# Where the activations begin in SBUF: one tile for both halves of hT, 80 bytes in front of the weights modulo 512

## The chip, the cores and the metric

The kernel runs on one core of a Trainium2 chip. The metric is the device time of one execution in microseconds. The times shown are medians over runs; a profile is one execution of the program, taken by the hardware profiler.

## The reference: what is computed

A decoder trunk of two layers over 512 positions of width 1024, all in float32. Layer 0 mixes positions with three groups of dilated attention heads, layer 1 with a gated linear recurrence (RG-LRU). Each mixer is followed by a gated FFN with a short causal convolution, and each of these four blocks has a norm ahead of it and one behind it.

```python
for layer in range(DEPTH):
    j = layer // 2
    h = rms_norm(x, norm_mix_pre[layer])
    if layer % 2 == 0:
        h = dilated_attention_mixer(h, attn_w_qkv[j], attn_w_o[j], rel_bias)
    else:
        h = rglru_mixer(h, lru_w_in[j], ...)
    x = x + rms_norm(h, norm_mix_post[layer])
    h = rms_norm(x, norm_ffn_pre[layer])
    h = conv_ffn(h, ffn_w_up[layer], ffn_conv_w[layer], ffn_conv_b[layer], ffn_w_down[layer])
    x = x + rms_norm(h, norm_ffn_post[layer])
```

## The kernel before

**Products in three parts.** Weights and activations are split into a rounded part and the rest (`hi`, `lo`, both of type fp32r), and `mm3` (lines 245 to 248) sums hi x hi, hi x lo and lo x hi into one bank of PSUM. Each line is one matmul with its own weight load; the profile shows the three as L246, L247 and L248. ScalarE makes `hi` and VectorE makes `lo` (lines 146 and 147).

**Which operand is which.** A matmul has a stationary operand (loaded first, 128 columns, 512 bytes of a partition) and a moving one (streamed, up to 512 columns, 2048 bytes). There are four kinds of three-part products, named by their PSUM tile:

- `ps`: projections of the normed activations (QKV, FFN up, LRU in). Stationary is a weight slice, moving is `hT`, the transposed activations. For the first four weight units of the two FFNs and of the LRU (four banks of PSUM each time) the 512 positions are taken in two halves of 256.
- `v`: the attention's values. Stationary is a slice of `hT`, moving is the weight.
- `acc`: the projections back (attention out, LRU out, FFN down). Stationary is a slice of an activation from the general pool, moving is the weight.
- `gate`: the LRU's gates. Stationary is a weight, moving an activation from the general pool.

Beside them the attention has plain fp32 products (`S`, `O`) and transposes (`tr`, `PT`, `OT`).

**Tiles and pools.** SBUF is handed out by pools, one behind the other in the order in which they are opened: `cp` (constants, x, gains, columns), `htp` (`hT`), `wp` (raw weights, and eight units of `hi` and `lo`), `gp` (28 general tiles of 2048 bytes), `sp` (small ones). `hT` is two tiles of 16384 bytes in a partition, one for `hi` and one for `lo`, with 8 slices of 512 positions each (line 278); one pair is live at a time, and each stage's pair takes the same place. All sizes ahead of the small tiles in `htp`, `wp` and `gp` are multiples of 512 bytes, so within these pools every slice that a matmul reads begins at the same place modulo 512.

**Order of the work.** Every engine's instructions stand in the order in which the program text writes them. A pump (`pump`, `load`) keeps three raw weight loads ahead on the SP queue and splits them into units as room comes free, between the matmul groups; the norms and the attention's softmax run as side steps between groups (`tick`).

Of the kernel before, what the change touches and what calls it, by code (L numbers as in the profile page):

```python
# [11 lines left out]
F32 = mybir.dt.float32  # L12
F32R = mybir.dt.float32r
# [5 lines left out]
P = 128  # L19
S = 512  # L20
D = 1024
KD = D // P
# [12 lines left out]
GEN_BUFS = 28  # L35
TOE_BUFS = 2
CP_PAD = 8

SHORT_ORDER = [
    ([0, 1], [0, 1, 2]), ([0], [3]), ([2, 3], [0]), ([1], [3]), ([2, 3], [1]), ([2], [2, 3]), ([3], [2, 3]),  # L40
# [36 lines left out]
def kernel(  # L77
# [31 lines left out]
    cp = ctx.enter_context(tc.tile_pool(name="cp", bufs=1))  # L109
    twice = cp.tile([P, CP_PAD], F32, tag="pad", name="pad")  # L110
    htp = ctx.enter_context(tc.tile_pool(name="htp", bufs=1))
    wp = ctx.enter_context(tc.tile_pool(name="wp", bufs=W_UNITS))
    gp = ctx.enter_context(tc.tile_pool(name="gp", bufs=GEN_BUFS))
    sp = ctx.enter_context(tc.tile_pool(name="sp", bufs=8))
    pp = ctx.enter_context(tc.tile_pool(name="pp", bufs=8, space=bass.MemoryType.PSUM))
    dp = ctx.enter_context(tc.tile_pool(name="dp", bufs=1, space=bass.MemoryType.DRAM))

    uid = [0]

    def nm(s):  # L120
        uid[0] += 1
        return f"{s}{uid[0]}"
# [152 lines left out]
        return [ap[:, 0:512], ap[:, 512:1024]]  # L275

    def new_hT():
        return tuple(htp.tile([P, KD, S], F32R, tag=f"hT{i}", name=nm(f"hT{i}")) for i in range(2))

    def prenorm(t, hT, g, wait):  # L280
        xh, gh = halves(x_sb[:, t, :]), halves(g)
# [126 lines left out]
    def rows_run(nchunks, A, prep, seq, order, post, pre):  # L408
        post_g = gain(*post)
        pre_g, hT = (gain(*pre), new_hT()) if pre is not None else (None, None)  # L410
        W, banks = {}, {}
        left = {}
# [95 lines left out]
    def ffn(layer, hT, post, pre):  # L508
        ca, cc = ffn_cols[layer]

        def conv(ps, j):
            u = gen(s="u")
            nc.scalar.activation(  # L513
                u, ps, AF.Identity, scale=cc[:, j : j + 1], bias=cc[:, 48 + j : 49 + j]
            )
            for d, wc in ((1, ca[:, 48 + j : 49 + j]), (2, ca[:, j : j + 1])):
                nc.vector.scalar_tensor_tensor(  # L517
                    u[:, d:], ps[:, : S - d], wc, u[:, d:], op0=ALU.mult, op1=ALU.add
                )
            return u  # L520

        gv = []

        def sink(b, ps, j):
            m = b % 2
            if b < 2:
                u = conv(ps, 2 * j + m)
                nc.scalar.activation(u, u, AF.Gelu_apprx_tanh)  # L528
                gv.append(u)
            else:  # L530
                u = conv(ps, 24 + 2 * j + m)
                nc.vector.tensor_tensor(gv[2 * j + m], gv[2 * j + m], u, op=ALU.mult)

        order = [([0, 1, 2, 3], range(9)), ([0], range(9, 12)), ([1], range(9, 12))]
        order += [([2, 3], [9]), ([2], [10, 11]), ([3], [10, 11])]
        prep, run = rows_proj(12, act_split(gv), order, post, pre)
        for j in range(12):
            if j == 11:
                prep(3)
            feat_tiles(2, hT, lambda b, ps: sink(b, ps, j), j == 0)  # L540
        return run()
# [408 lines left out]

    root_table()
    hT = new_hT()
    nc.sync.dma_start(x_sb[:, 0, :], x[0, 0:P, :])
    g = gain(norm_mix_pre, 0, nc.sync)
# [27 lines left out]
    hT = attention(hT, (norm_mix_post, 0), (norm_ffn_pre, 0))  # L982
    hT = ffn(0, hT, (norm_ffn_post, 0), (norm_mix_pre, 1))
    hT = lru(hT, (norm_mix_post, 1), (norm_ffn_pre, 1))
# [30 lines left out]
```

## Time and profile before

| | |
|---|---|
| median of 3 runs | 1498.67 us (1498.09 to 1500.18) |
| the profiled execution's own time | 1498.71 us |
| its span, first to last instruction | 1496.9 us |
| mean granted TensorE clock | 0.997 |
| TensorE, VectorE, ScalarE busy | 1474.0, 795.3, 633.7 us |
| matmuls in the trace | 7083 |
| weight load of 1 MB, issue to landing | 5.2 us |
| fp32r matmuls that read hT | 4128 of 512 columns, 576 of 256 |

A group's line in the profile reads: line, engine, operation, output<-inputs, shapes, count | busy us, mean ns of one | idle time ahead of them and what ended it. A row of the timeline reads: start in us, length in us, engine, line, operation, names, shapes, count. Matmuls overlap, so their lengths add up to more than the time they take; the distance from start to start is what one costs. A window's row gives the length of a stretch, then each engine's busy time with its count of instructions, the granted clock, the DMA share and GB/s.

### The profile page before, as it was taken

How to read it: one execution, taken by the hardware profiler on the slowest of the kernel's cores; microseconds unless marked ns; L12 is line 12 of the kernel's file. 1: busy time of each engine (PE TensorE's matmuls, PEld its weight loads, DVE VectorE, ACT ScalarE, POOL GpSimd, SP SyncE). 2: the span in 40 equal slices, each digit the busy share in tenths (PEclk: the TensorE clock that was granted, in tenths of full speed). 3: DMA queues.
4: the chain of work that ended last, by engine and by line, in shares of the span. 5: the costliest groups of instructions: out<-in, count | busy, mean ns of one | idle time of the engine just before them, and what ended most of it. 6: DMA issues, size and time to landing. Idle time of an engine off the chain costs nothing.

```text
span 1496.9 us, 18111 instructions
## 1 busy us (share of the span) xinstructions
PE 1474.0 (98%) x7083; PEld 1237.8 (83%) x7083; DVE 795.3 (53%) x1612; ACT 633.7 (42%) x1287; POOL 43.7 (3%) x73
## 2 busy tenths in 40 slices
PE   6999999999999999999999999999999999999998
PEld 4788888888888898888888888988898888888886
DVE  6434334343434586555555336877876555565333
ACT  5334333333334554333344334579554333344321
POOL 3111000000000000000000000000000000000000
PEclk9999999999999999999999999999999999999999
DMA  6543222423334233323233231342233232323301
GB/s 215 184 164 98 92 88 85 133 100 125 107 121 137 95 110 119 106 87 111 85 113 113 85 113 43 99 142 84 85 99 113 92 105 87 110 85 116 109 1 56
DMA packets 116101, 157.64 MB, mean 105 GB/s; under 512 B 5087, under 2 KB 97463, under 8 KB 116016
## 3 DMA queue, kind: packets, MB, share of 16 engines
q1 hardware_dynamic: 111120, 145.24, 29.3%
q0 software_dynamic: 4896, 11.26, 2.3%
q8 instruction: 55, 0.90, 0.3%
q14 instruction: 30, 0.25, 0.0%
HBM read 150.14 MB, written 11.05 MB: 108 GB/s over the span
## 4 chain that ended last, share of the span: by engine, by line
PE 88%; ACT 5%; DVE 4%; DMA 2%; issue 1%; SPq 0%; POOL 0%; DVEq 0%; ACTq 0%; POOLq 0%
PE ps L246 17%; PE ps L248 17%; PE ps L247 17%; PE acc L248 7%; PE acc L246 7%; PE acc L247 7%; PE v L246 3%; PE v L247 3%; PE v L248 3%; DVE wlo L147 2%; DVE xb L838 1%; ACT whi L146 1%; PE S L714 1%; PE tr L297 1%; PE O L772 1%; PE O L699 1%
## 5 line engine op out<-in xcount | busy, mean ns | idle before, releaser
L246 PE MATMUL ps<-hT,whi 128*128 128x512 f32 (+1 forms) x1376 | 518.5, 377 | 0.0
L248 PE MATMUL ps<-hT,wlo 128*128 128x512 f32 (+1 forms) x1376 | 515.2, 374 | 0.0
L247 PE MATMUL ps<-hT,whi 128*128 128x512 f32 (+1 forms) x1376 | 515.1, 374 | 0.0
L147 DVE TENSOR_TENSOR wlo<-raw,whi 128x512 fp32r<-128x512 f32 x504 | 328.1, 697 | 270.3 <-ACT whi L146 270.1
L146 ACT ACTIVATE whi<-raw 128x512 fp32r<-128x512 f32 x504 | 285.2, 623 | 135.0 <-PE acc L248 120.9
L246 PEld LDWEIGHTS ps<-hT,whi 128*128 128x128 f32 x1376 | 259.1, 188 | 47.0 <-ACT qk L590 0.6
L248 PEld LDWEIGHTS ps<-hT,wlo 128*128 128x128 f32 x1376 | 259.0, 188 | 46.5
L247 PEld LDWEIGHTS ps<-hT,whi 128*128 128x128 f32 x1376 | 259.1, 188 | 45.6
L517 DVE SCALAR_TENSOR_TENSOR u<-ps,cols,u 128x511 f32<-128x511 f32 x192 | 143.8, 749 | 140.4 <-ACT u L513 137.0
L248 PE MATMUL acc<-whi,alo 128*128 128x512 f32 x512 | 199.4, 389 | 1.0 <-DVE alo L147 1.0
L246 PE MATMUL acc<-whi,ahi 128*128 128x512 f32 x512 | 200.0, 391 | 0.0
L247 PE MATMUL acc<-wlo,ahi 128*128 128x512 f32 x512 | 199.2, 389 | 0.0
L513 ACT ACTIVATE u<-ps,cols 128x512 f32<-128x512 f32 x96 | 74.8, 780 | 209.9 <-PE ps L248 209.9
L248 PEld LDWEIGHTS acc<-whi,alo 128*128 128x128 f32 x512 | 96.1, 188 | 21.4 <-DVE alo L147 1.4
L246 PEld LDWEIGHTS acc<-whi,ahi 128*128 128x128 f32 x512 | 96.1, 188 | 19.7
L247 PEld LDWEIGHTS acc<-wlo,ahi 128*128 128x128 f32 x512 | 96.1, 188 | 19.6
L246 PE MATMUL v<-whi,hT 128*128 128x512 f32 x192 | 78.3, 408 | 0.0
L247 PE MATMUL v<-wlo,hT 128*128 128x512 f32 x192 | 76.5, 398 | 1.4 <-DVE wlo L147 1.4
L248 PE MATMUL v<-whi,hT 128*128 128x512 f32 x192 | 76.3, 398 | 0.5 <-DVE hT L302 0.5
L528 ACT ACTIVATE u<-u 128x512 f32<-128x512 f32 x48 | 30.3, 632 | 80.6 <-DVE u L517 80.6
L651 DVE CUSTOM_DVE_ANT_0 L<-S,toe 128x128 f32<-128x128 f32 (+1 forms) x96 | 25.2, 320 | 53.4 <-DMA toe<-skew 22.7
L590 ACT ACTIVATE qk<-ps 128x512 f32<-128x512 f32 x24 | 14.3, 597 | 88.7 <-PE ps L248 76.9
(169 smaller groups left out, 1028.5 us busy)
## 6 DMA issues: line engine op xcount, KB each, us to landing
raw<-in_ffn_w_up_dram SPq DMA_DIRECT2D x48, 1024.0 KB, 5.2
raw<-in_attn_w_qkv_dram SPq DMA_DIRECT2D x28, 1024.0 KB, 5.1
raw<-in_ffn_w_down_dram SPq DMA_DIRECT2D x24, 1024.0 KB, 4.9
raw<-in_attn_w_qkv_dram SPq DMA_DIRECT2D x16, 512.0 KB, 4.9
raw<-in_lru_w_in_dram SPq DMA_DIRECT2D x8, 1024.0 KB, 5.4
skew<-rowv POOLq DMA_DIRECT2D x3, 1536.0 KB, 12.3
vrows<-v SPq DMA_DIRECT2D x16, 256.0 KB, 2.8
vp<-vrows SPq DMA_DIRECT2D x16, 256.0 KB, 4.0
```

What stands on the lines that cost most here:

```text
L146: nc.scalar.activation(hi, raw, AF.Copy)
L147: nc.vector.tensor_tensor(lo, raw, hi.bitcast(F32), op=ALU.subtract)
L246: mm(dst, l[0], r[0], start=start, stop=False)
L247: mm(dst, l[0], r[1], start=False, stop=False)
L248: mm(dst, l[1], r[0], start=False, stop=stop)
L297: nc.tensor.transpose(ps[:, k * P : (k + 1) * P], xs[i][:, k * P : (k + 1) * P], ident)
L513: nc.scalar.activation(u, ps, AF.Identity, scale=cc[:, j : j + 1], bias=cc[:, 48 + j : 49 + j])
L517: nc.vector.scalar_tensor_tensor(u[:, d:], ps[:, : S - d], wc, u[:, d:], op0=ALU.mult, op1=ALU.add)
L528: nc.scalar.activation(u, u, AF.Gelu_apprx_tanh)
L651: nc.vector.tensor_tensor_reduce(dst, ps, bias, scale=1.0, scalar=3 * NEG, op0=ALU.add, op1=ALU.max, accum_out=mx)
L699: mm(po[:, a * P : (a + 1) * P], pts[a, j], vtile(v, a - 1 + j, h % 4), start=j == js[0], stop=j == 1)
L714: mm(ps[:, c], q[hh][:, c], k[hh][:, c], start=True, stop=True)
```

## The change

`new_hT` makes one tile for both halves, 32 bytes (8 floats) longer than the two together, and uses it from byte 16 (`HT_AT` = 4 floats); the two halves are views into it. A tile `wpad` of 64 bytes, which nothing reads or writes, is put at the head of the pool `wp`.

```diff
+HT_AT = 4
...
+    wp.tile([P, 16], F32, tag="wpad", name="wpad", bufs=1)
...
     def new_hT():
-        return tuple(htp.tile([P, KD, S], F32R, tag=f"hT{i}", name=nm(f"hT{i}")) for i in range(2))
+        both = htp.tile([P, 2 * KD * S + 8], F32R, tag="hT", name=nm("hT"))[:, HT_AT : HT_AT + 2 * KD * S]
+        both = both.rearrange("p (i k s) -> p i k s", i=2, k=KD)
+        return both[:, 0], both[:, 1]
```

In the built programs the tiles begin at these places in a partition (bytes; in brackets modulo 512):

| tile | before | after |
|---|---|---|
| ident, x_sb, gains (pool `cp`) | 16544 and up (160) | the same |
| hT, hi half | 44608 (64) | 44624 (80) |
| hT, lo half | 60992 (64) | 61008 (80) |
| first raw weight | 77376 (64) | 77472 (160) |
| first `hi` unit | 101952 (64) | 102048 (160) |
| first general tile | 167488 (64) | 167584 (160) |

Everything behind hT moves by 96 bytes, hT itself by 16. The instructions, their order on each engine and their semaphore waits are the same in both programs.

## The prediction

> **What bounds the kernel now.** I read the page first (engine shares, clock, chain), then the waits of TensorE, then the groups of matmuls by form, and last the timeline of single matmuls, because the change touches nothing but where operands begin in SBUF.
>
> ```profile
> span 1496.9 us, 18111 instructions
> PE 1474.0 (98%) x7083; PEld 1237.8 (83%) x7083; DVE 795.3 (53%) x1612; ACT 633.7 (42%) x1287; POOL 43.7 (3%) x73
> PE 88%; ACT 5%; DVE 4%; DMA 2%; issue 1%; SPq 0%; POOL 0%; DVEq 0%; ACTq 0%; POOLq 0%
> ...
> PE tr L297 <- ACT xs L330: 10.4, 1, 10.4
> PE v L247 <- DVE wlo L147: 1.4, 2, 0.7
> ```
>
> TensorE is busy for 98% of the span and holds 88% of the chain that ends last; its longest wait (10.4 us) happens once, while the kernel starts. So the kernel's time is the number of matmuls times the distance from one matmul's start to the next one's. These are the groups that carry it:
>
> ```profile
> L246 PE MATMUL ps<-hT,whi 128*128 128x512 f32 x1184 | 463.7, 392 | 0.0
> ...
> L246 PE MATMUL acc<-whi,ahi 128*128 128x512 f32 x512 | 200.0, 391 | 0.0
> ...
> L246 PE MATMUL v<-whi,hT 128*128 128x512 f32 x192 | 78.3, 408 | 0.0
> ...
> L246 PE MATMUL ps<-hT,whi 128*128 128x256 f32 x192 | 54.8, 285 | 0.0
> ```
>
> Each line is one of three (L246, L247, L248) with the same count. The 392 ns are a matmul's length, not its price: successive matmuls overlap. The price is read from starts, here the first and last of 138 rows without a break, and the first and last of 88 rows of the 256-column form:
>
> ```profile
> 619.80 0.39 PE L248 MATMUL ps<-hT,wlo 128*128 128x512 f32 x1
> ...
> 650.85 0.39 PE L247 MATMUL ps<-hT,whi 128*128 128x512 f32 x1
> ...
> 551.52 0.28 PE L248 MATMUL ps<-hT,wlo 128*128 128x256 f32 x1
> ...
> 561.96 0.28 PE L248 MATMUL ps<-hT,wlo 128*128 128x256 f32 x1
> ```
>
> 31.05 us over 137 steps is 226.6 ns per 512 columns; 10.44 us over 87 steps is 120.0 ns per 256 columns. The second 256 columns cost 106.6 ns, so 512 columns are 213.3 ns of streaming and both forms carry the same 13.3 ns on top. That 13.3 ns, once per matmul and its weight load, is all that a change of addresses can touch. Is it fixed? Two views say that it is not. First, a stretch in which the clock was halved:
>
> ```profile
> 26.50:28.00 1.50, 1.50 (x5) 1.24 (x4) 1.09 (x5) 0.28 (x2) 0.00 (x0) 0.50 0.11 33
> ...
> 26.85 0.63 PE L248 MATMUL v<-whi,hT 128*128 128x512 f32 x1
> ...
> 28.13 0.54 PE L248 MATMUL v<-whi,hT 128*128 128x512 f32 x1
> ```
>
> At a granted clock of 0.50 the step is 1.28 us over 3, or 426.7 ns: exactly twice 213.3, with no extra at all. The same holds for the fp32 products, which take their columns at half speed:
>
> ```profile
> 106.07 1.52 PE S L664 x8
> ...
> 240.14 1.78 PE S L714 x16
> ```
>
> L714 holds 16 records of 128 columns, 0.111 us each. L664 holds two such and six of 256 columns: (1.52 - 0.22) / 6 is about 0.216 us, 3 ns over 213.3. So where the moving operand is read at half speed the weight load beside it is nearly free; at full speed it costs 13.3 ns. The second view is what happens after a break:
>
> ```profile
> 34.59 0.40 PE L247 MATMUL v<-wlo,hT 128*128 128x512 f32 x1
> 34.82 0.40 PE L248 MATMUL v<-whi,hT 128*128 128x512 f32 x1
> 35.06 0.40 PE L246 MATMUL v<-whi,hT 128*128 128x512 f32 x1
> 35.29 0.40 PE L247 MATMUL v<-wlo,hT 128*128 128x512 f32 x1
> 35.53 0.39 PE L248 MATMUL v<-whi,hT 128*128 128x512 f32 x1
> 35.75 0.39 PE L246 MATMUL v<-whi,hT 128*128 128x512 f32 x1
> 35.98 0.40 PE L247 MATMUL v<-wlo,hT 128*128 128x512 f32 x1
> 36.22 0.39 PE L248 MATMUL v<-whi,hT 128*128 128x512 f32 x1
> 36.45 0.40 PE L246 MATMUL v<-whi,hT 128*128 128x512 f32 x1
> 36.68 0.39 PE L247 MATMUL v<-wlo,hT 128*128 128x512 f32 x1
> 36.91 0.39 PE L248 MATMUL v<-whi,hT 128*128 128x512 f32 x1
> ```
>
> The steps here are 0.23, 0.24, 0.23, 0.24, 0.22, 0.23, 0.24, 0.23, 0.23, 0.23 (in the trace's nanoseconds from 224 to 236) before they settle at 227. Operands, sizes and offsets modulo 512 are those of the steady state; only the timing of the two reads against each other differs. So the gap depends on how the weight read and the moving read lie against each other. That is a lever that an address offset can move, in either direction.
>
> **The change part by part.** Removed and added instructions: none. On all five engines the changed program has the same instructions in the same order with the same semaphore waits; only start addresses differ. The terms:
>
> 1. *Matmuls that gain an offset.* The projections over hT (ps) have hT moving and the weights stationary, and the value products (v) the reverse. By the counts above that is 3 x 1184 + 3 x 192 = 4128 of 512 columns and 3 x 192 = 576 of 256: 4704 matmuls. Before, both operands begin at 64 modulo 512; after, hT begins at 80 and the weights at 160.
>
> 2. *Matmuls that gain none.* The acc products (3 x 512) and the LRU gates take the activation from the general pool; these tiles move by 96 bytes exactly like the weights, so their operands still begin alike. Price 0. If the absolute place counted instead, these 1536 would be worth 1.5 us per ns.
>
> 3. *What a nanosecond is worth.* TensorE never waits for long in the stages concerned:
>
> ```profile
> 560.00:900.00 340.00, 340.00 (x1519) 282.25 (x1518) 182.94 (x272) 134.51 (x227) 0.00 (x0) 1.00 0.31 103
> 960.00:1060.00 100.00, 99.53 (x442) 81.92 (x440) 78.41 (x119) 78.15 (x126) 0.00 (x0) 1.00 0.34 109
> ```
>
> In the first FFN VectorE is busy for 183 of 340 us and ScalarE for 135, so a step shorter by 5% stays fed. The LRU stage (960 to 1060) is tighter, 78 of 100 us on both, and might give back a part of its few us. So 4704 matmuls make 4.7 us per ns.
>
> The bounds of that term. Best: the gap falls to what the fp32 products leave, 216 ns instead of 226.6, 10.6 ns less: 4704 x 10.6 = 50 us. Worst among the steps seen after a break: 236 ns, 9.4 ns more: 4128 x 9.4 = 39 us. The trace has no f32r matmul with operands that begin at different places, so I take the nearest rows, the steps after a break: the best of them, 224 ns, is the one in which the two reads happened to lie better, 2.7 ns less than the steady 226.6. 4704 x 2.7 = 12.7 us. I choose this end of the two because the two regimes without a gap show that the 13.3 ns is a clash and not work, and because operands that begin alike and are read at the same speed are the likeliest to stay in step. I don't take the whole 50 us, because no full-speed step in the trace comes near 216.
>
> [...]
>
> 4. *Other operands.* ScalarE, VectorE and the DMAs now address tiles at 160 modulo 512 instead of 64. The trace has both kinds already: gain and x_sb begin at 160.
>
> ```profile
> L285 DVE TENSOR_TENSOR xs<-x_sb,gain 128x512 f32<-128x512 f32 x24 | 16.2, 683 | 0.0
> ...
> L866 DVE TENSOR_TENSOR xb<-xb,sig 128x512 f32<-128x512 f32 x8 | 5.1, 684 | 0.0
> ...
> raw<-in_ffn_w_up_dram SPq DMA_DIRECT2D x48, 1024.0 KB, 5.2
> ```
>
> 683 ns against 684 ns: 0. A weight load of 1 MB lands in 5.2 us and feeds 48 matmuls, 10.9 us at 226.6 ns, with three buffers; if the new place made it slower by half it would still be hidden. If that cover were gone, the difference would appear as TensorE waiting for wlo.
>
> The sum: the profiled execution took 1498.71 us (span 1496.9 and 1.8 around it), practically the median of 1498.67. 1498.7 - 12.7 + 0 + 0 = **1486.0 us**, 0.8% less.
>
> **The rivals.**
>
> *The whole gap goes.* With 80 bytes between them the two reads never meet, as at half clock: 216 ns and 109 ns. 1498.7 - 50 = 1448.7. For it: the regimes without a gap, and the same 13.3 ns at 256 and 512 columns, as if the load always met the stream in full. Against it: full-speed steps never went under 224.
>
> *Nothing moves.* The gap belongs to the load itself, an amount that a stream at half speed hides and one at full speed can't, wherever the operands begin; the uneven steps after a break are the order in which loads are dispatched. Then 1498.7, within 0.2% either way (about what a measurement of this kernel can tell from no change). For it: ps, acc and v, whose operands lie in quite different pools, all keep 226.6, and the steady state is always reached again. [...] Against it: it must explain by chance why the gap after a break swings by 12 ns. That the change does not do what it says I rule out: the start addresses are in the program.
>
> *It settles at a worse step.* The steady 226.6 is a phase that the equal starts allow; the ten steps after the break take 2.32 us, 232 ns on average. If hT at 80 bytes holds the projections in such a phase, the place is every ps and v matmul, and the price is 4128 x (232 - 226.6) = 22 us, so 1521; at 236 throughout it is 39 us, so 1537. It decides from the point where the steady step exceeds 227.3 ns (0.2% of 1498.7, 3 us, over 4704 matmuls).
>
> **How the numbers follow.** A part of the gap goes (1475 to 1495): 0.36. The whole gap goes (about 1449): 0.18. Nothing moves: 0.25. A worse step: 0.21. So faster 0.54, same 0.25, slower 0.21. The predicted time is that of the first case, 1486; its own range is 1475 to 1495. To leave out no more than two in ten the range goes down over the whole gap, to 1447, and up over no change and the mildest slower step (1 ns, 5 us), to 1504.
>
> **What would show it.** In the profile after, take two far rows of ps matmuls within a stretch like 619 to 651 and divide by the steps: 224 ns would bear out the forecast, 216 the first rival, 226.6 the second, more the third. The acc matmuls must keep 226.6; if they change too, the absolute place counts and term 2 is wrong. The ps matmuls of 256 columns should show the same difference per matmul as those of 512, if the gap is paid per weight load. The v matmuls carry the offset the other way round (the weights moving, hT stationary); they may differ from ps, and at 576 they are worth 0.6 us per ns. The lengths on VectorE and the loads' 5.2 us should stay; a new wait of TensorE for wlo would mean that the splits can't follow. The prediction is wrong if ps steps at 226.6 or more.

## The result: slower by 1.3%

The changed kernel takes 1518.98 us (1518.0 to 1519.96) against 1498.4 us for the kernel before in the same comparison: a ratio of 1.0134, 95% interval 1.0119 to 1.0150. The prediction was 1486 us with a range up to 1504. What came is its third rival, a worse step, which had been priced at 1521 us and given a chance of 0.21.

### The profile page after: what moved, and what is told of

Same layout as the page of the kernel before. It is cut to its first block, busy times and chain, and to the rows that moved or that the text cites. A ratio compares the mean times of both kernels' runs of the same rounds, so it can differ in the third digit from the quotient of the medians.

```text
span 1517.5 us, 18111 instructions
## 1 busy us (share of the span) xinstructions
PE 1495.4 (99%) x7083; PEld 1236.3 (81%) x7083; DVE 795.2 (52%) x1612; ACT 634.2 (42%) x1287; POOL 43.6 (3%) x73
## 4 chain that ended last, share of the span: by engine, by line
PE 98%; DVE 1%; DMA 0%; ACT 0%; issue 0%; DVEq 0%; SPq 0%
PE ps L251 20%; PE ps L250 20%; PE ps L249 20%; PE acc L251 8%; PE acc L249 8%; PE acc L250 8%; PE v L249 3%; PE v L250 3%; PE v L251 3%; PE O L777 1%; PE S L719 1%; PE tr L302 1%; PE O L704 1%; PE S L669 1%; DVE wlo L150 1%; PE gate L250 0%
## 5 line engine op out<-in xcount | busy, mean ns | idle before, releaser
L251 PE MATMUL ps<-hT,wlo 128*128 128x512 f32 (+1 forms) x1376 | 524.2, 381 | 0.0
L249 PE MATMUL ps<-hT,whi 128*128 128x512 f32 (+1 forms) x1376 | 522.6, 380 | 0.0
L250 PE MATMUL ps<-hT,whi 128*128 128x512 f32 (+1 forms) x1376 | 522.3, 380 | 0.0
L249 PEld LDWEIGHTS ps<-hT,whi 128*128 128x128 f32 x1376 | 258.7, 188 | 53.7 <-ACT qk L595 0.6
L251 PEld LDWEIGHTS ps<-hT,wlo 128*128 128x128 f32 x1376 | 258.3, 188 | 52.0
L249 PE MATMUL acc<-whi,ahi 128*128 128x512 f32 x512 | 200.1, 391 | 0.0
L251 PE MATMUL acc<-whi,alo 128*128 128x512 f32 x512 | 199.5, 390 | 0.0
L251 PEld LDWEIGHTS acc<-whi,alo 128*128 128x128 f32 x512 | 96.1, 188 | 20.4 <-DVE alo L150 0.3
L249 PEld LDWEIGHTS acc<-whi,ahi 128*128 128x128 f32 x512 | 96.1, 188 | 19.7
L249 PE MATMUL v<-whi,hT 128*128 128x512 f32 x192 | 78.5, 409 | 0.2 <-ACT hT L306 0.2
L251 PE MATMUL v<-whi,hT 128*128 128x512 f32 x192 | 76.2, 397 | 0.0
```

The source lines that it names most:

```text
L249: mm(dst, l[0], r[0], start=start, stop=False)
L250: mm(dst, l[0], r[1], start=False, stop=False)
L251: mm(dst, l[1], r[0], start=False, stop=stop)
```

## The profile after

The page of the changed kernel, engine shares and chain, and the waits of TensorE (the lines are numbered three to five higher than before; L249 to L251 are the three matmuls of `mm3`):

```profile
span 1517.5 us, 18111 instructions
PE 1495.4 (99%) x7083; PEld 1236.3 (81%) x7083; DVE 795.2 (52%) x1612; ACT 634.2 (42%) x1287; POOL 43.6 (3%) x73
PE 98%; DVE 1%; DMA 0%; ACT 0%; issue 0%; DVEq 0%; SPq 0%
...
PE tr L302 <- ACT xs L335: 10.4, 1, 10.4
PE v L250 <- DVE wlo L150: 2.7, 4, 0.7
```

The span grew by 20.6 us and TensorE's busy time by 21.4, with the same 7083 matmuls. VectorE and ScalarE have the times of before, and all waits of TensorE together are 14.6 us against 15.4. No wait grew that could explain the loss; each matmul of 512 columns over hT takes longer. (TensorE's share of the chain rises from 88% to 98%: in the LRU, where the chain before ran mainly through VectorE and ScalarE, it now runs through the matmuls.) The timeline of ps, in the first FFN, the first and the last of 133 rows without a break:

```profile
620.01 0.40 PE L250 MATMUL ps<-hT,whi 128*128 128x512 f32 x1
...
650.81 0.40 PE L250 MATMUL ps<-hT,whi 128*128 128x512 f32 x1
```

30.80 us over 132 steps is 233.3 ns, against 226.6 before. The back projections of the same kernel, 141 rows without a break, did not change:

```profile
860.05 0.39 PE L249 MATMUL acc<-whi,ahi 128*128 128x512 f32 x1
...
891.78 0.39 PE L251 MATMUL acc<-whi,alo 128*128 128x512 f32 x1
```

31.73 us over 140 steps, 226.6 ns. Adding up every distance from one matmul's start to the next, by PSUM tile, gives the whole account against the trace of before: ps of 512 columns +20.6 us, v +1.7, acc -0.9, ps of 256 columns -0.3, all others together -0.4. The sum is the 20.6 us of the span.

The longer step isn't a uniform one. It comes in a fixed cycle of three:

```profile
700.05 0.40 PE L251 MATMUL ps<-hT,wlo 128*128 128x512 f32 x1
700.28 0.39 PE L249 MATMUL ps<-hT,whi 128*128 128x512 f32 x1
700.51 0.40 PE L250 MATMUL ps<-hT,whi 128*128 128x512 f32 x1
700.75 0.40 PE L251 MATMUL ps<-hT,wlo 128*128 128x512 f32 x1
```

In the trace's nanoseconds the steps of both FFNs repeat 236, 229, 235 (the first from L251) with a sum of 700 ns. In the attention the same cycle begins at another of the three lines (236 from L249), and the LRU runs at another step, 231 ns on average, with the same addresses modulo 512.

## The experiments

Two theories at the start. **P, place:** hT begins at 80 modulo 512, which is 16 modulo 32, and a moving operand off a 32-byte boundary costs extra. **D, distance:** what counts is how far apart the moving and the stationary operand of a matmul begin, modulo some length; the places themselves don't matter. "Distance" is below the number of bytes by which hT begins in front of the weights, modulo 512: in ps by which the moving operand begins in front of the stationary one. In v, where the roles are exchanged, the moving operand begins behind by the same number.

### Without the filler: distance 16

```diff
-    wp.tile([P, 16], F32, tag="wpad", name="wpad", bufs=1)
```

> The changed kernel without the 64-byte filler ahead of the weights: hT still begins at 80 modulo 512, the weights at 96, so 16 bytes apart instead of 80. Theory P (place: a hT that begins off a 32-byte boundary, at 16 modulo 32, costs extra, whatever the weights do): the ps step stays at 233 ns, time 1519 us. Theory D (distance between the two starts modulo 512 decides): the ps step changes; being close to equal starts it should lie nearer to 227 ns, time 1495 to 1510 us.

1520.82 us against 1499.31, ratio 1.0147 (1.0132 to 1.0162). In the first FFN, 134 rows from first to last:

```profile
619.85 0.40 PE L249 MATMUL ps<-hT,wlo 128*128 128x512 f32 x1
...
650.88 0.40 PE L247 MATMUL ps<-hT,whi 128*128 128x512 f32 x1
```

31.03 us over 133 steps, 233.3 ns: as P had it, and D's guess that 16 bytes would be near to equal starts was wrong. In the attention the mean of the same kernel's ps steps is 236.1 ns. The v matmuls of the same trace, whose moving operand begins 16 bytes behind the stationary one, don't pay this. The first and last of 47 rows without a break, the last ones before a group of ps:

```profile
35.52 0.39 PE L248 MATMUL v<-wlo,hT 128*128 128x512 f32 x1
...
45.95 0.39 PE L249 MATMUL v<-whi,hT 128*128 128x512 f32 x1
```

10.43 us over 46 steps, 226.7 ns. The next rows are ps matmuls over the same hT, and their steps are at 233 ns at once.

### HT_AT = 0: distance 96, hT where it was

```diff
-HT_AT = 4
+HT_AT = 0
```

> The changed kernel with HT_AT = 0: hT begins at 64 modulo 512, as before the change and on a 32-byte boundary; the weights stay at 160, so 96 bytes apart. Theory P: the ps step is back at 227 ns and the time at 1498 us. Theory D: the step is not 227 ns; 96 lies next to 80, so about 230 to 236 ns, 1510 to 1525 us. If the weights' place at 160 alone did it (theory W), the step stays at 233 ns, but the acc step, whose operands both lie at 160 after the change and which stayed at 227 ns, speaks against W.

1524.27 us, ratio 1.0172 (1.0155 to 1.0189), the slowest of all. 133 rows from first to last:

```profile
619.84 0.40 PE L250 MATMUL ps<-hT,whi 128*128 128x512 f32 x1
...
650.77 0.39 PE L250 MATMUL ps<-hT,whi 128*128 128x512 f32 x1
```

30.93 us over 132 steps, 234.3 ns, with hT at the very place that it had before. P is refuted: a hT on a 32-byte boundary, at its old place, pays as much as the shifted one.

### The sweep: one distance for each stage

hT is made anew for each of four stages, so that one kernel can hold four distances. The tile gets 104 floats (416 bytes) of room and each stage begins at its own offset in it; the filler is taken out. The weights then begin at 480 modulo 512. Of the five kernels the first differs from the changed one by:

```diff
-HT_AT = 4
+HT_AT = [100, 96, 92, 88]
+HT_EXT = 104
...
-    wp.tile([P, 16], F32, tag="wpad", name="wpad", bufs=1)
...
+    stage = [0, 1, 2, 3]
+
     def new_hT():
-        both = htp.tile([P, 2 * KD * S + 8], F32R, tag="hT", name=nm("hT"))[:, HT_AT : HT_AT + 2 * KD * S]
+        at = HT_AT[stage.pop(0)]
+        both = htp.tile([P, 2 * KD * S + HT_EXT], F32R, tag="hT", name=nm("hT"))[:, at : at + 2 * KD * S]
```

The others differ in the four numbers alone (104 minus a quarter of the distance).

> One distance for each stage: the weights begin at 480 modulo 512 and hT begins 16 (attention), 32 (first FFN), 48 (LRU) and 64 (second FFN) bytes in front of them. Read by stage from the starts of the ps matmuls of 512 columns. Theory P: 233 ns at 16 and 48 (hT at 16 modulo 32), 227 ns at 32 and 64. Theory D: four different steps between 224 and 236 ns, changing smoothly with the distance. No effect of distance or place: 227 ns in all four.

> The same with 96 (attention), 128 (first FFN), 256 (LRU) and 384 (second FFN) bytes; every hT begins on a 32-byte boundary. Theory P: 227 ns in all four stages. [...]

> The sweep's runs so far gave, in the stages' steady state, 226.7 ns for ps of 512 columns at distances 0 and 256, and 233.3 to 234.7 ns at 16, 32, 48, 64, 80, 96, 128 and 384 bytes. Here 4 (attention), 8 (first FFN), 240 (LRU) and 272 (second FFN) bytes. Theory D256 (only a multiple of 256 bytes between the two starts keeps the two reads out of each other's way, everything else costs alike): 233 to 235 ns in all four. Rival G (the cost grows with the distance from a multiple of 256): nearer to 227 at 4 and 8. Rival S (the sign matters: the value products, in which the weights move and begin behind hT by 16 bytes, kept 227 ns): 227 ns at 240, where the stationary weights begin 16 bytes ahead of a multiple of 256, 233 ns at 272.

> Distances 32 (attention), 192 (first FFN), 224 (LRU) and 320 (second FFN) bytes. Theory D256: 233 to 235 ns in all four. Rival S: 227 ns or less at 192 and 224 (64 and 32 bytes short of a multiple of 256), 233 ns at 32 and 320. A period of 64 bytes: 227 ns at 192 and 320, which the 233 ns at 64, 128 and 384 speak against already.

> Distances 144 (attention), 160 (first FFN), 208 (LRU) and 176 (second FFN) bytes, around the one distance besides 0 and 256 that came near the old step (192: 228.9 ns on average). Theory D256: 229 to 235 ns, none below 226.7, so no place of hT makes the kernel faster than before. Rival (a dip between 144 and 208): a step below 226.7 ns, which would be worth 4.1 us per ns for a kernel with that distance.

The times of these kernels (1521.52, 1522.92, 1520.86, 1515.08 and 1517.78 us, one run each) mix four distances and say little. The steps, each the mean over all steps under 260 ns of ps of 512 columns in a stage (about 1100 in attention, 1055 in an FFN, 285 in the LRU), say more:

| distance, bytes | step, ns (stage) |
|---|---|
| 0 (before) | 226.7 (FFN) |
| 4, 8 | 230.8 (attention), 232.0 (FFN) |
| 16 | 233.3 (FFN), 236.1 (attention) |
| 32, 64 | 233.3, 233.3 (FFN) |
| 48 | 234.7 (LRU) |
| 80 (the change) | 233.3 (FFN), 231.4 (LRU), 232.9 (attention) |
| 96 | 234.3 (FFN) |
| 128, 160 | 233.3, 233.3 (FFN) |
| 144 | 230.8 (attention) |
| 176 | 231.1 (FFN) |
| 192 | 228.9 (FFN) |
| 208, 224, 240 | 232.8, 233.4, 231.6 (LRU) |
| 256 | 226.8 (LRU) |
| 272 | 236.7 (FFN) |
| 320, 384 | 233.3, 233.3 (FFN) |

For ps only 0 and 256 keep 226.7 ns; 4 bytes are enough to lose over 3 ns (the attention's means hold its many breaks; before it was 227.4 there). A smooth rise from equal starts (rival G) didn't come: 4 and 8 bytes lie between, but from 16 on there is a level at 233.3 with strays to 228.9 and 236.7. The sign rival S is refuted for ps by 240 and 224. The one distance that came near, 192, is the first FFN of the fourth kernel of the sweep, 136 rows from first to last:

```profile
619.89 0.39 PE L250 MATMUL ps<-hT,wlo 128*128 128x512 f32 x1
...
650.79 0.39 PE L250 MATMUL ps<-hT,wlo 128*128 128x512 f32 x1
```

30.90 us over 135 steps, 228.9 ns, in a cycle of 232, 226, 229. None of the distances tried goes under 226.7 on average, so the dip that the last kernel of the sweep looked for, around 192, isn't there.

The value products of the same traces are a second row of distances, with the moving operand behind. The mean of their steps from the eleventh after each break on (about 285 in a kernel) is 226.7 ns at equal starts, 233.3 with 4 bytes, 227.4 and 227.1 with 16 (the kernel without the filler and the first of the sweep; both settle at 226.7), 233.3 with 32, 230.1 with 80 (the change), and 233.3 with 96 and 144. So an unequal start doesn't always cost something: 16 bytes in front cost ps 6.6 ns or more in both kernels, 16 bytes behind cost v less than 1 ns in the same two. Neither the number of bytes alone nor its sign gives the step, and no run tells why 16 bytes behind are nearly free.

### The same for the general pool

Here the kernel before is left as it is but for a filler that moves the general tiles by 96 bytes. hT isn't touched.

```diff
+    gp.tile([P, 24], F32, tag="gpad", name="gpad", bufs=1)
```

> The kernel before, with a filler of 96 bytes at the head of the general pool and nothing else: hT and the weights begin alike as before (64 modulo 512), the general tiles at 160. The back projections (acc) then have a stationary operand that begins 96 bytes behind the moving weights, the gates a moving operand 96 bytes behind the stationary weights. Theory D256: ps and v stay at 227 ns, acc rises as ps did at 96 bytes, to about 234 ns, and the kernel takes 1536 x 7.6 ns = 11.7 us more, 1511 us. If only the operand hT mattered (its size, its being one tile): acc stays at 227 ns, 1499 us.

1509.99 us against 1498.18, ratio 1.0082 (1.0065 to 1.0099), 11.8 us more. 137 rows of each kind, first and last, of this kernel:

```profile
619.98 0.39 PE L249 MATMUL ps<-hT,whi 128*128 128x512 f32 x1
...
650.80 0.39 PE L250 MATMUL ps<-hT,wlo 128*128 128x512 f32 x1
...
860.02 0.39 PE L250 MATMUL acc<-whi,alo 128*128 128x512 f32 x1
...
891.89 0.39 PE L248 MATMUL acc<-whi,ahi 128*128 128x512 f32 x1
```

The projections over hT stay at 30.82 / 136 = 226.6 ns, and the back projections rise to 31.87 / 136 = 234.3 ns: the same number to a tenth that ps had at 96 bytes, with other operands, other pools, and the roles exchanged (here the weights move and begin 96 bytes in front of the stationary activations). By starts, acc alone accounts for +10.5 us of this trace's 10.2. The LRU's gates, whose moving operand now begins 96 bytes behind the stationary weights, go from 227.0 to 233.6 ns on average. So it is the distance between the two operands of a matmul that makes the step longer, and not something about hT; how much longer differs with the stage and with which operand is in front.

### One half of hT in front, the other not

The lo half begins like the weights and the hi half 96 bytes in front of them, or the reverse, in turn from stage to stage:

```diff
+        n, two = KD * S, stage.pop(0) % 2
+        both = htp.tile([P, 2 * n + HT_EXT], F32R, tag="hT", name=nm("hT"))
+        far, near = (
+            both[:, i : i + n].rearrange("p (k s) -> p k s", k=KD) for i in (HT_EXT - 24, n + HT_EXT)
+        )
+        return (near, far) if two else (far, near)
```

> Only one half of hT lies 96 bytes in front of the weights, the other begins like them: in the FFNs the lo half (moving in the second of the three matmuls), in attention and LRU the hi half (moving in the first and the third). Theory of pairs (a matmul whose moving operand clashes with the weight load that runs beside it pays for itself): in the FFNs only the step from the second matmul grows, to about 234 ns or by up to 23 ns if it must pay the three matmuls' 7.6 ns alone, the others keep 227, mean 229 to 234 ns; in attention and LRU the other way round, mean 232 ns. Rival (the stream as a whole gets out of step): all three steps grow alike in all stages, mean 234 ns.

1517.25 us in its one run. The first FFN, where only the second matmul of three (L248) has a moving operand at 96, 134 rows from first to last:

```profile
619.94 0.40 PE L249 MATMUL ps<-hT,wlo 128*128 128x512 f32 x1
...
650.82 0.40 PE L247 MATMUL ps<-hT,whi 128*128 128x512 f32 x1
```

30.88 us over 133 steps, 232.2 ns. In nanoseconds the cycle is 236, 228, 229, 234, 233, 233, beginning with a step from L247: all three lines got longer, the step that ends at L248's start (from L247, 236 and 234) the most and the one from L248 (228 and 233) the least. In attention and LRU, where two of three have the distance, the mean is 232.3 and 232.2 ns. So one matmul of three at an unequal distance costs as much as two of three, and 5.5 of the 7.6 ns that all three cost. Pairs that pay for themselves would have left two lines at 227; that is refuted. The rival, that all lines grow alike, is nearer, but its 234 ns in all three didn't come either: by line the cycle's steps are 235, 230.5 and 231 ns on average (from L247, L248 and L249). How a distance in one matmul makes the steps of the other two longer no run tells.

### Distance 256 in all stages

```diff
-HT_AT = 4
+HT_AT = 40
...
-    wp.tile([P, 16], F32, tag="wpad", name="wpad", bufs=1)
...
-        both = htp.tile([P, 2 * KD * S + 8], F32R, tag="hT", name=nm("hT"))[:, HT_AT : HT_AT + 2 * KD * S]
+        both = htp.tile([P, 2 * KD * S + 104], F32R, tag="hT", name=nm("hT"))[:, HT_AT : HT_AT + 2 * KD * S]
```

> The common tile as in the change, without the filler, hT beginning exactly 256 bytes in front of the weights modulo 512 in all stages (hT at 224, weights and general tiles at 480). Theory D256: ps, v and acc all step at 226.7 ns and the time is that of the kernel before, 1498 us, though every address has moved and the two halves lie in one tile. If the common tile or the new places themselves cost anything, the time lies above 1500 us.

1498.75 us against 1498.31, ratio 1.0002 (0.9993 to 1.0011). 138 rows from first to last:

```profile
619.89 0.39 PE L249 MATMUL ps<-hT,wlo 128*128 128x512 f32 x1
...
650.94 0.39 PE L248 MATMUL ps<-hT,whi 128*128 128x512 f32 x1
```

31.05 us over 137 steps, 226.6 ns. Every tile from hT on has moved and both halves lie in one tile, and nothing is lost. So the common tile, the slice at an offset and the new places cost nothing; the whole loss of the change is its distance of 80 bytes.

## Why the prediction was wrong, point by point

**What bounds the kernel: right.** Time is the number of matmuls times their step; what the ps and v matmuls lost the kernel lost, but for 1.7 us. The terms at nothing were right as well: other operands (VectorE 795.2 us as before, 1 MB loads 5.2 us) and acc (226.6 ns). The common tile, which the sum doesn't name, costs nothing either (distance 256).

**That a step depends on how the two operands lie against each other: right.** It is shown for the distance between their starts: with hT 80 bytes in front of the weights the ps step went from 226.6 to 233.3 ns, with the general tiles moved by 96 bytes the acc step went from 226.6 to 234.3, and at 256 bytes ps was back at 226.6. That the 13.3 ns are a clash of two reads was my inference; the traces show starts and lengths of instructions, not the reads. That an offset can move the step "in either direction" isn't shown either: none of the distances tried goes under 226.7 ns on average, the step at equal starts.

**The term's sign and size: wrong.** The step that failed is "The bounds of that term": of the ends 216 and 236 ns I chose 224, because operands that begin alike and are read at the same speed seemed to me the likeliest to stay in a clash; no trace had shown that. It measured 233.3 ns in the FFNs. The runs show the reverse: equal starts (226.7 ns) and starts 256 bytes apart (226.8) settle at the shortest mean step found, and of the other starts all settle at longer ones (ps 228.9 to 236.7, v 230.1 to 233.3) but v at 16 bytes, which settles at the same one (226.7). The steps after a break, which I had used as a sample of what an offset can do, had pointed this way by their mean (232 ns), and I took their best one, 224, instead. No distance tried holds the stream at that single short step: at 192 bytes a cycle even holds one of 226 ns and averages 228.9. The two ends weren't counted alike either: the 50 us at the good end are for all 4704 matmuls, the 39 us at the bad end for the 4128 of 512 columns.

**The third rival: right in place and total, the price in part by luck.** It put the stream in a phase like those after a break, with 4128 x 5.4 = 22 us on ps and v of 512 columns. These two measured 20.6 + 1.7 = 22.3 us, and the rest gave back 1.7. Its condition (a steady step above 227.3) was met. But its one price for both hides two misses that cancel: ps lost 5.8 ns per matmul and v 3.0. That the longer step is the phase seen after a break isn't shown: after a break the steps wander between 224 and 236 ns and settle at 226.7, here they repeat in a cycle, and other distances settle anywhere from 226.7 to 236.7.

**The other rivals.** The whole gap goes: it needed 216 ns, and none of the distances tried goes under 226.7 ns on average. Nothing moves: refuted, as the step of these fp32r matmuls goes from 226.6 to 233.3 ns by the distance of the operands alone.

**The 256-column matmuls and v** I had priced like the others. v came out smaller, 230 ns against 227.5, about half per matmul. The 256-column form went the other way: 120.1 ns instead of 120.7. So what the change costs isn't a fixed amount per weight load, as the equal 13.3 ns of both forms had suggested.

**Open.** What it is in the distance that makes a step longer no run tells, nor why the same distance costs differently in different stages (80 bytes: 233.3 ns in the FFNs, 231.4 in the LRU), and next to nothing in v at 16 bytes. That it is the distance between the moving and the stationary operand rather than that between successive moving ones rests on successive moving operands of one kind beginning alike in all kernels but that with split halves. Whether the 13.3 ns that by my estimate are left at equal starts can be had by other means is open too; by an offset of hT at the distances tried it can't.

## What to carry to other kernels

Where fp32r matmuls of 512 columns run back to back, try first to let the moving and the stationary operand begin alike, or 256 bytes apart, modulo 512. Here these two gave 226.7 and 226.8 ns, and every other distance tried cost the projections over hT 1% to 4.5% of the step. A filler tile or a resized pool can do that by accident: the 96 bytes at the head of the general pool cost 11.8 us. (v with 16 bytes lost less than 1 ns; it is the one exception found.) When steps after a break wander before they settle, don't price a term by the best of them: here their mean (232 ns) lay nearer to the outcome (233.3) than their best (224), though it doesn't give the step of every distance. A parameter that can differ by stage lets one run measure four settings, if the quantity is read from the trace and not from the total time.

## What the runs showed that I had not expected

The effect depends on the width of the moving operand. At a distance of 16 bytes the 512-column steps grew from 226.7 to 233.3 ns, while the 256-column ones became shorter. Of the kernel without the filler, the first and last of 52 rows without a break:

```profile
561.94 0.28 PE L247 MATMUL ps<-hT,whi 128*128 128x256 f32 x1
...
567.92 0.28 PE L247 MATMUL ps<-hT,whi 128*128 128x256 f32 x1
```

5.98 us over 51 steps is 117.2 ns, against 120.0 before. At 576 matmuls that is 1.6 us, too little to pay for anything here.

Some distances have more than one step for ps: 16 bytes gave 236.1 ns in the attention, in two kernels alike, and 233.3 in the FFNs and the LRU of one of them; 80 bytes gave 233.3 in the FFNs and 231.4 in the LRU. And the transposes, which take 0.87 us for eight of 128 columns (109 ns each, where fp32r takes 120 ns for 256), show no effect at the one distance tried: their operands lay 96 bytes apart before (ident at 160, the general tiles at 64 modulo 512) and begin alike after the change, and eight of them take 0.87 us in both. From the chain of before, and then of after:

```profile
524.25 0.87 PE tr L297 x8
```

```profile
530.89 0.87 PE tr L302 x8
```
